# Two-layer hybrid encoder step: most gate products of the merge taken in pairs by seven half products instead of eight

## The chip, the cores and the metric

The kernel runs on one core of one Trainium2 chip. The metric is the device time of one execution in microseconds (us), the median of several runs.

## The reference

One step of a streaming encoder with two layers, on 640 tokens (512 of a prompt, 8 samples of 16) of width 1024, everything in fp32. Cut to what matters here:

```
z = x @ w_in            # 54 blocks of 128 columns are used feature-major below
oa = gelu(u) * (mix_w @ v + b) * silu(a_g)      # chunked spatial gating
ob = rglru(conv4(b_x)) * silu(b_g)              # gated linear recurrence
oc = latent_attention(...) * silu(c_g)
om = memory_attention(m_q, mem_k, mem_v)
g = sigmoid(gate_logits)                        # 4 x 1024 columns of z
merged = g0 * (oa @ w_a) + g1 * (ob @ w_b) + g2 * (oc @ w_c) + g3 * (om @ w_m)
x = layer_norm(ALPHA * x + merged @ w_out)
```

The sigmoid is computed as 0.5 * (1 + tanh(0.5 * logit)). The gate logits are 32 of the 54 column blocks of a layer, each a product of 1024 by 128 weights with 1024 by 640 activations.

## The kernel before

**Arithmetic.** Every large operand is split into two reduced-precision parts, h and lo: ACT casts it (line 145), DVE subtracts the cast from the original (line 146). Each product then takes three matmuls per 128 rows of the contraction: h with h, h with lo, lo with h. `fm_product` (line 116) issues them, each for the two halves of the 640 tokens (TH = 320 columns). A gate chunk thus has 8 x 3 x 2 = 48 matmuls of 128 x 320, all issued at line 120.

**Weights.** `wload` (line 108) sends a DMA from SP's queue into a tile `raw` (three slots of 1024 columns), and ACT and DVE split it into `wh` and `wl` (two slots for each size).

**Order of work in a layer.** Projections `c` and `v`, keys and values of the memory (`mem_kv`, line 210), q, k and v of the attention, attention with the mixing of the gating branch placed among its matmuls (line 623), memory attention, the recurrence (lines 734 to 799: convolution, gates, scan), then the merge, then the output projection (line 953) and the layer norm. A scheduler fills each engine's queue at build time from the order of the code and of the tile slots; an engine runs its queue strictly in order. Waits arise from tiles: a write waits for the readers of the slot or tile, and a tile counts as one, also where two operations touch different halves of it.

**The merge** (`merge`, line 853) runs over the branches oa, oc, ob and om, and in each over 8 output blocks f. For each f: `fm_chunk` (48 matmuls), tanh on ACT (line 865), the branch's own product `y` (24 matmuls of 320 columns, 12 for om), then on DVE the product of gate and branch (lines 877 and 881). For the second to fourth branch it is added to the sum `macc` (line 884), by POOL for oc and ob and by DVE for om. The first four chunks of oa are interleaved with the recurrence. The lines that set the merge's order:

```
for f in range(8):
    o = fm_chunk(22 + br * 8 + f)
    g = ftmp([128, T], "g")
    ACT.activation(out=halves(g), in_=o, func=AF.Tanh, scale=0.5)
    wh, wl = wload(ins["w_brm"][l, f] if br == 3 else ins["w_br"][l, br, f], nk * 128)
```

Of the kernel before, what the change touches and what calls it, by code (L numbers as in the profile page):

```python
# [16 lines left out]
D = 1024  # L17
# [23 lines left out]
def encoder_step(  # L41
# [19 lines left out]
    def xtile(name):  # L61
        return xp_.tile([128, 4, T], F32R, tag="x", name=name)
# [40 lines left out]
    def wraw(src, n=1024):  # L103
        raw = wp.tile([128, n], F32, tag="raw", name="raw", bufs=3)
        nc.sync.dma_start(out=raw, in_=src)
        return raw

    def wload(src, n=1024):
        raw = wraw(src, n)
        sz = "" if n > 512 else "2"  # L110
        h = wp.tile([128, n], F32R, tag="wh" + sz, name="wh")
        lo = wp.tile([128, n], F32R, tag="wl" + sz, name="wl")
        split(h, lo, raw)
        return h, lo

# [12 lines left out]
    def tm_products(outs_, lhs_h, lhs_l, nc_, nk_per, width, load):  # L128
        for ci in range(nc_):
            wh, wl = load(ci)  # L130
            steps = [(j, a, wh) for j in range(nk_per) for a in (lhs_h, lhs_l)]
            steps += [(j, lhs_h, wl) for j in range(nk_per)]
            for n, (j, a, w) in enumerate(steps):
                for t, o in enumerate(outs_):
                    PE.matmul(  # L135
                        out=o[:, 0:width],
                        lhsT=a(ci * nk_per + j)[:, t * 128:(t + 1) * 128],
                        rhs=w[:, j * width:(j + 1) * width],
                        start=(ci == 0 and n == 0),
                        stop=(ci == nc_ - 1 and n == len(steps) - 1),  # L140
                    )
# [33 lines left out]
    xscr = dr.tile([T, D], F32, name="xscr")  # L175

    for l in range(L):
# [12 lines left out]
        mh = kvtile([128, KD, 256], F32R, "mem_h")  # L190
        ml = kvtile([128, KD, 256], F32R, "mem_l")
        def mem_in(k):
            mt = wraw(ins["memT"][:, k:k + 4, :].rearrange("p a b -> p (a b)"))
            for m in range(2):
                split(
                    mh[:, k + 2 * m:k + 2 * m + 2, :], ml[:, k + 2 * m:k + 2 * m + 2, :],
                    mt[:, m * 512:(m + 1) * 512].rearrange("p (a b) -> p a b", a=2),
                )

        def w_mem(c):  # L200
            r = wload(ins["w_mem"][l, c])
# [42 lines left out]
        def w_c(c):  # L244
            if l > 0:
                return wload(ins["w_c"][l, c], 832)
            if c > 0:
                r = wload(ins["w_c"][l, c], 832)
                x_in(2 * c, 2)
                return r  # L250
            raw = wp.tile([128, 832], F32, tag="raw", name="raw", bufs=3)
            h = wp.tile([128, 832], F32R, tag="wh", name="wh")
            lo = wp.tile([128, 832], F32R, tag="wl", name="wl")
            for j in range(2):
                js = slice(416 * j, 416 * j + 416)
                nc.sync.dma_start(out=raw[:, js], in_=ins["w_c"][l, c][:, js])
                x_in(j, 1)
                split(h[:, js], lo[:, js], raw[:, js])
            return h, lo
# [7 lines left out]
        def fm_chunk(c, l=l):  # L267
            h, lo = wload(ins["w_fm"][l, c])
            o = acc("fm")
            fm_product(  # L270
                o,
                lambda k: h[:, k * 128:(k + 1) * 128],
                lambda k: lo[:, k * 128:(k + 1) * 128],
                xhk, xlk, KD,
            )
            return o[:, :, 0:TH]

# [29 lines left out]
        def w_v(c):  # L307
            r = wload(ins["w_v"][l, c])
# [46 lines left out]
        sc = stile([128, 5120], F32, "sc")  # L355
        ckvT_s = sc[:, 0:1152].rearrange("p (b k) -> p b k", b=NB)
        krT_s = sc[:, 1152:2304].rearrange("p (b k) -> p b k", b=NB)
        past = sc[:, 2304:3328].rearrange("p (b k) -> p b k", b=NB)
        qa = sc[:, 3328:4352].rearrange("p (b k) -> p b k", b=NB)
        qrs = sc[:, 4352:4864].rearrange("p (b k) -> p b k", b=NB)  # L360
# [3 lines left out]
        nc.sync.dma_start(out=past, in_=ins["past_ckv"][l].rearrange("b k c -> k b c"))  # L364

# [59 lines left out]
        def q_product(o, wh, wl, m):  # L425
            fm_product(
                o,
                lambda k: wh[:, (2 * m + k) * 128:(2 * m + k + 1) * 128],
                lambda k: wl[:, (2 * m + k) * 128:(2 * m + k + 1) * 128],
# [3 lines left out]
        wh, wl = wload(ins["w_uqr"][l], 512)  # L433
# [17 lines left out]
        wh, wl = wload(ins["w_uqn"][l])  # L451
# [18 lines left out]
        wh, wl = wload(ins["w_ukv"][l])  # L470
        for hp in range(4):
            o = bank_s("k_ps")
            ms = slice(hp * 128, (hp + 1) * 128)
            for n, (a, b) in enumerate(((wh, ckh), (wl, ckh), (wh, ckl))):
                PE.matmul(out=o, lhsT=a[:, ms], rhs=b, start=(n == 0), stop=(n == 2))
# [3 lines left out]
        for t in range(4):  # L479
            o = bank_s("v_ps")  # L480
            ts_ = slice(t * 128, (t + 1) * 128)
            for n, (a, b) in enumerate(((ckh, wh), (ckh, wl), (ckl, wh))):
                PE.matmul(out=o, lhsT=a[:, ts_], rhs=b[:, 512:1024], start=(n == 0), stop=(n == 2))
            (DVE.tensor_copy if t % 2 else ACT.copy)(out=vc[:, t, :], in_=o)

# [72 lines left out]
        for i in range(4):  # L558
# [42 lines left out]
            )  # L601

# [1 line left out]
        for c in range(4):  # L604
# [4 lines left out]
        wmx = stile([128, 1536], F32, "wmx")  # L609
        ws_p = wmx[:, 0:512].rearrange("p (g q) -> p g q", g=4)  # L610
        ws_s = wmx[:, 512:1024].rearrange("p (g q) -> p g q", g=4)
        bs = wmx[:, 1024:1536].rearrange("p (g q) -> p g q", g=4)
        nc.sync.dma_start(out=wmx[:, 0:1024], in_=ins["w_mix"][l])
        nc.sync.dma_start(out=wmx[:, 1024:1536], in_=ins["rows"][l:l + 1, 1024:1536].partition_broadcast(128))
        wm = wmx[:, 0:1024].rearrange("p (g q) -> p g q", g=8)
        POOL.affine_select(
            out=wm, in_=wm, pattern=[[0, 8], [1, 128]],
            compare_op=ALU.is_ge, fill=0.0, base=0, channel_multiplier=-1,
        )
        for c in range(4):  # L620
            o = acc("mix").rearrange("p a b -> p (a b)")
            for t in range(NT):
                PE.matmul(  # L623
                    out=o[:, t * 128:(t + 1) * 128], lhsT=v[:, t, c * 128:(c + 1) * 128],
                    rhs=(ws_p if t < 4 else ws_s)[:, c, :], start=True, stop=True,
                )
            th = ftmp([128, T], "mixb")
            DVE.tensor_tensor(
                out=th[:, 0:NP_].rearrange("p (a b) -> p a b", a=4),
                in0=o[:, 0:NP_].rearrange("p (a b) -> p a b", a=4),  # L630
                in1=bs[:, c:c + 1, :].to_broadcast([128, 4, 128]), op=ALU.add,
            )
            DVE.tensor_tensor(
                out=th[:, NP_:T].rearrange("p (a b) -> p a b", a=NB),
                in0=o[:, NP_:T].rearrange("p (a b) -> p a b", a=NB),
                in1=bs[:, c:c + 1, 0:TS].to_broadcast([128, NB, TS]), op=ALU.add,
            )
            DVE.tensor_tensor(out=oa[:, c, :], in0=oa[:, c, :], in1=th, op=ALU.mult)
# [142 lines left out]
        def lru_rest(c):  # L781
# [17 lines left out]
            DVE.tensor_tensor(out=obs, in0=obs, in1=samp(lb[c % 2][:, 1, :])[:, :, 0:TS], op=ALU.mult)  # L799

# [49 lines left out]
        macc = atile([128, 8, T], F32, "macc")  # L850
        mgh, mgl = [], []

        def merge(bi):
            src, nk, scale = ((oa, 4, 0.5), (oc, 4, 0.5), (ob, 4, 0.5), (om, 2, 1.0))[bi]
            br = (0, 2, 1, 3)[bi]
            bhl = stile([128, 2, nk, T], F32R, "bhl")
            for k in range(nk):
                split(bhl[:, 0, k, :], bhl[:, 1, k, :], src[:, k, :], scale)
            if bi == 3:
                mgh.extend(otile([128, 4, T], F32R, f"mgh{i}") for i in range(2))  # L860
                mgl.extend(otile([128, 4, T], F32R, f"mgl{i}") for i in range(2))
            for f in range(8):
                o = fm_chunk(22 + br * 8 + f)
                g = ftmp([128, T], "g")
                ACT.activation(out=halves(g), in_=o, func=AF.Tanh, scale=0.5)  # L865
                wh, wl = wload(ins["w_brm"][l, f] if br == 3 else ins["w_br"][l, br, f], nk * 128)
                y = acc("y")
                fm_product(
                    y,
                    lambda k: wh[:, k * 128:(k + 1) * 128],  # L870
                    lambda k: wl[:, k * 128:(k + 1) * 128],
                    lambda k: bhl[:, 0, k, :], lambda k: bhl[:, 1, k, :], nk,
                )
                y = y[:, :, 0:TH]
# [233 lines left out]
```

## Time and profile before

| | |
|---|---|
| device time, median of 3 runs (lowest, highest) | 1449.41 us (1448.57, 1450.07) |
| span of the profiled execution, first to last instruction | 1446.2 us |
| median over that span | 3.2 us |
| granted TensorE clock over the span | 0.998 of full |
| busy share PE, PE weight loads, DVE, ACT, POOL | 99%, 91%, 49%, 37%, 10% |
| share of PE in the chain that ended last | 93% |
| DMA, mean | 93 GB/s |

PE is the matmul engine TensorE, DVE is VectorE, ACT ScalarE, POOL GpSimd, SP SyncE, whose queue issues most DMAs. A busy PE says only that matmuls were in flight: they are pipelined, so what one costs is the distance between two starts, not its own duration. The chain that ended last is followed back from the last instruction to what released each step.

### The profile page before, as it was taken

Reading aid. Unit: us, or ns where it says so; the run is one execution under the profiler, and the core shown is the slowest. Engines: PE = TensorE matmul, PEld = TensorE weight load, DVE = VectorE, ACT = ScalarE, POOL = GpSimd, SP = SyncE. Lnnn points to the kernel's source line nnn. Section 1 sums busy time; section 2 is a strip of 40 time slices with the busy share of each in tenths; the row PEclk is TensorE's granted clock in tenths of the full one; section 3 lists DMA queues with packets and bytes.
Section 4 is the critical chain, followed back from the end, with each engine's and each line's share of the span. In section 5 each row is a group of like instructions: output and inputs, shape, how many; then the busy total and the mean of one; then the engine's idle time right before and its main releaser. Section 6 shows DMA issues by size and latency. Waiting matters only on the chain.

```text
span 1446.2 us, 22712 instructions
## 1 busy us (share of the span) xinstructions
PE 1426.0 (99%) x9376; PEld 1322.8 (91%) x9376; DVE 709.0 (49%) x1264; ACT 530.9 (37%) x931; POOL 138.7 (10%) x200
## 2 busy tenths in 40 slices
PE   8999999999999999999999999999999999999997
PEld 8899888989999999998898998788899999999986
DVE  5643577386542232444834535763954322323546
ACT  5533443265532232333234434432664222222320
POOL 2020000010101112100111100000111011211000
PEclk9999999999999999999999999999999999999999
DMA  8342113213222222134372222032132222222323
GB/s 288 115 142 74 52 36 111 78 59 111 74 80 73 81 73 77 61 101 156 115 229 92 85 73 66 30 117 81 48 121 69 73 81 73 81 64 73 114 73 110
DMA packets 51065, 134.16 MB, mean 93 GB/s; under 512 B 5777, under 2 KB 14897, under 8 KB 49937
## 3 DMA queue, kind: packets, MB, share of 16 engines
q1 hardware_dynamic: 49328, 127.54, 27.7%
q0 software_dynamic: 1632, 5.16, 1.0%
q8 instruction: 74, 1.21, 0.4%
q14 instruction: 31, 0.25, 0.1%
HBM read 123.59 MB, written 7.78 MB: 91 GB/s over the span
## 4 chain that ended last, share of the span: by engine, by line
PE 93%; DVE 4%; ACT 1%; DMA 1%; issue 1%; DVEq 0%; POOL 0%; SPq 0%; ACTq 0%
PE fm L120 52%; PE y L120 14%; PE y_ps L953 6%; PE v L135 4%; PE c L135 3%; PE sc_ps L568 3%; PE pv_ps L592 2%; PE mem L135 2%; PE q_ps L120 1%; PE pt_ps L585 1%; PE gate L773 1%; PE mix L623 1%; PE ss_ps L513 1%; DVE wl L146 1%; PE ptm_ps L831 1%
## 5 line engine op out<-in xcount | busy, mean ns | idle before, releaser
L146 DVE TENSOR_TENSOR wl<-raw,wh 128x1024 fp32r<-128x1024 f32 (+4 forms) x203 | 206.0, 1016 | 419.4 <-issue 288.8
L120 PE MATMUL fm<-xh,wh 128*128 128x320 f32 x1728 | 406.9, 313 | 0.0
L120 PE MATMUL fm<-xl,wh 128*128 128x320 f32 x1728 | 404.1, 312 | 0.0
L145 ACT CAST wh<-raw 128x1024 fp32r<-128x1024 f32 (+4 forms) x203 | 179.2, 883 | 477.6 <-PE fm L120 326.8
L120 PEld LDWEIGHTS fm<-xh,wh 128*128 128x128 f32 x1728 | 289.3, 188 | 8.3 <-issue 5.0
L120 PEld LDWEIGHTS fm<-xl,wh 128*128 128x128 f32 x1728 | 289.6, 188 | 5.6 <-issue 4.9
L120 PE MATMUL fm<-xh,wl 128*128 128x320 f32 x1728 | 281.0, 311 | 0.0
L120 PEld LDWEIGHTS fm<-xh,wl 128*128 128x128 f32 x1728 | 258.7, 188 | 3.4 <-issue 2.6
L120 PE MATMUL y<-bhl,wh 128*128 128x320 f32 x896 | 141.6, 309 | 0.0
L120 PEld LDWEIGHTS y<-bhl,wh 128*128 128x128 f32 x896 | 133.6, 188 | 0.0
L884 POOL TENSOR_TENSOR macc<-macc,g 128x640 f32<-128x640 f32 x32 | 62.1, 1941 | 340.5 <-DVE g L881 340.5
L881 DVE SCALAR_TENSOR_TENSOR g<-g,y 128x640 f32<-128x640 f32 x48 | 39.4, 821 | 95.8 <-PE y L120 95.8
L120 PE MATMUL y<-bhl,wl 128*128 128x320 f32 x448 | 76.6, 309 | 0.0
L865 ACT ACTIVATE g<-fm 128x640 f32<-128x640 f32 x64 | 45.2, 706 | 81.4 <-PE fm L120 81.3
L120 PEld LDWEIGHTS y<-bhl,wl 128*128 128x128 f32 x448 | 68.3, 188 | 0.0
L568 PE MATMUL sc_ps<-kT,qT 128*128 128x128 f32 (+7 forms) x128 | 45.6, 450 | 0.0
L577 ACT ACTIVATE p_c<-sc_ps,mx 128x128 f32<-128x128 f32 (+3 forms) x64 | 33.6, 532 | 4.5 <-DVE mx L574 4.5
L953 PE MATMUL y_ps<-wo,mgh 128*128 128x512 f32 x120 | 35.1, 396 | 0.0
L587 ACT COPY pt_c<-pt_ps 128x128 f32<-128x128 f32 (+3 forms) x32 | 13.6, 425 | 52.8 <-PE pt_ps L585 52.8
L574 DVE TENSOR_REDUCE mx<-sc_ps 128x1 f32<-128x128 f32 (+3 forms) x64 | 30.3, 477 | 0.5
L585 PE MATMUL pt_ps<-ident,p_c 128*128 128x128 f32 x160 | 28.4, 275 | 1.7 <-DVE pt_c L587 1.7
L585 PEld LDWEIGHTS pt_ps<-ident,p_c 128*128 128x128 f32 x160 | 19.9, 140 | 10.8 <-issue 4.3
(295 smaller groups left out, 1675.2 us busy)
## 6 DMA issues: line engine op xcount, KB each, us to landing
raw<-in_w_fm SPq DMA_DIRECT2D x108, 512.0 KB, 3.5
raw<-in_w_br SPq DMA_DIRECT2D x48, 256.0 KB, 2.6
mcache<-in_mem_kv SPq DMA_DIRECT2D x8, 1024.0 KB, 4.8
raw<-in_w_out SPq DMA_DIRECT2D x16, 512.0 KB, 4.3
raw<-in_w_v SPq DMA_DIRECT2D x8, 512.0 KB, 4.0
raw<-in_w_mem SPq DMA_DIRECT2D x8, 512.0 KB, 3.5
raw<-in_w_c SPq DMA_DIRECT2D x7, 416.0 KB, 5.1
xr<-in_x SPq DMA_DIRECT2D x10, 256.0 KB, 3.0
```

The source lines that it names most:

```text
L120: PE.matmul(out=out[:, j, 0:TH], lhsT=a(k), rhs=b(k)[:, j * TH:(j + 1) * TH], start=(n == 0), stop=(n == len(steps) - 1),)
L135: PE.matmul(out=o[:, 0:width], lhsT=a(ci * nk_per + j)[:, t * 128:(t + 1) * 128], rhs=w[:, j * width:(j + 1) * width], start=(ci == 0 and ...
L145: ACT.copy(out=dst_h, in_=src)
L146: DVE.tensor_tensor(out=dst_l, in0=src, in1=dst_h.bitcast(F32), op=ALU.subtract)
L568: PE.matmul(out=s[:, 0:nk], lhsT=qT[0:kr_, h, ts_], rhs=kT[h // 4][0:kr_, h % 4, 0:nk], start=True, stop=True,)
L574: DVE.tensor_reduce(out=mx, in_=s[:, 0:nk], axis=AX.X, op=ALU.max, negate=True)
L577: ACT.activation(out=p[:, 0:nk], in_=s[:, 0:nk], func=AF.Exp, bias=mx, accum_out=sm)
L585: PE.transpose(tps[:, k * 128:(k + 1) * 128], p[:, k * 128:(k + 1) * 128], ident)
L865: ACT.activation(out=halves(g), in_=o, func=AF.Tanh, scale=0.5)
L881: DVE.scalar_tensor_tensor(out=halves(g), in0=halves(g), scalar=1.0, in1=y, op0=ALU.add, op1=ALU.mult)
L884: (POOL if bi < 3 else DVE).tensor_tensor(out=m, in0=m, in1=g, op=ALU.add)
L953: PE.matmul(out=o[j], lhsT=a[k // 4][:, k % 4, t * 128:(t + 1) * 128], rhs=w[:, j * 512:(j + 1) * 512], start=(k == 0 and p == 0), stop=(k ...
```

## The change

The gate chunks 4 to 7 of oa and all of oc, ob and om (28 of 32 in a layer) are computed two at a time by `fm_pair` (line 309 of the changed kernel). Two chunks form a 2 x 2 block matrix: the rows are the two chunks, the columns the two halves of the contraction (4 x 128 each). The activations form another: halves of the contraction by halves of the tokens. Instead of eight half products (each 12 matmuls of 320 columns) it makes seven, from sums of weight blocks (`wsum`, 4 DVE additions of 512 columns for a pair) and of activation blocks (`x_sums` and `x_sum_in_place`, DVE, once a layer, in the recurrence's stage), and five DVE operations of 320 columns on the results in PSUM (lines 356, 358, 362, 364 and 367).

```
         def fm_pair(c, take):
             a11, a12, a21, a22 = (
                 wraw(ins["w_fm"][l, c + e][:, i * 512:(i + 1) * 512]) for e in range(2) for i in range(2)
             )
...
+            product(ba, a11, 11, True, False)
+            ACT.copy(out=p1, in_=ba)
+            s1 = wsum(a21, a22, "ws1")
+            s2 = wsum(a11, s1, "ws2")
+            product(bb, s2, 2, True, True)
+            DVE.tensor_tensor(out=u, in0=p1, in1=bb, op=ALU.subtract)
+            product(bc, wsum(a11, a21, "ws3"), 3, True, False)
+            DVE.tensor_tensor(out=z1[:, hi_], in0=bc, in1=u, op=ALU.subtract)
+            product(ba, a12, 21, False, True)
+            take(0, lo_, ba)
+            product(bd, s1, 1, True, False)
+            DVE.tensor_tensor(out=z1[:, hi_], in0=z1[:, hi_], in1=bd, op=ALU.subtract)
+            product(bc, a22, 4, False, True)
+            DVE.tensor_tensor(out=z1[:, lo_], in0=bc, in1=u, op=ALU.subtract)
+            take(1, slice(0, T), z1)
+            product(bd, wsum(a12, s2, "ws4"), 22, False, True)
+            DVE.tensor_tensor(out=z0[:, hi_], in0=bd, in1=u, op=ALU.add)
+            take(0, hi_, z0[:, hi_])
```

`product` splits its weight block (ACT cast, DVE subtraction, 512 columns) and issues 12 matmuls. `ba` and `bb` lie in one PSUM tile, `bc` and `bd` in another.

The other edits: the weights come in pieces of 512 columns and 256 KB (`raw` six slots, `wh` and `wl` four each, sums `ws` four); the addition to `macc` is on DVE for all branches; oc, ob and om are written to DRAM by DMAs from SP's queue (`spill`) and read back for their branch's first pair (`back`, tile `osrc`); activations, branch results and others share one pool of ten slots; the output projection's weights are loaded in halves; and the mixing moves from the attention to the stage ahead of the q products.

```
+    def spill(bi, k, src):
+        nc.sync.dma_start(out=oscr[bi][k], in_=src)
...
+        def x_sums():
...
+            for k in range(4):
...
+                x_sum1(k, t1, t2)
+                DVE.tensor_tensor(out=t2, in0=t1, in1=b22[0], op=ALU.add)
+                DVE.tensor_tensor(out=t2, in0=t2, in1=b22[1], op=ALU.add)
+                split(xt[2][0][:, k, :], xt[2][1][:, k, :], t2)
+                DVE.tensor_tensor(out=t4, in0=b21[0], in1=t2, op=ALU.subtract)
+                DVE.tensor_tensor(out=t4, in0=t4, in1=b21[1], op=ALU.add)
+                split(xt[4][0][:, k, :], xt[4][1][:, k, :], t4)
+                DVE.tensor_tensor(out=t3, in0=b12[0], in1=b22[0], op=ALU.subtract)
+                DVE.tensor_tensor(out=t1, in0=b12[1], in1=b22[1], op=ALU.subtract)
+                DVE.tensor_tensor(out=t3, in0=t3, in1=t1, op=ALU.add)
+                split(xt[3][0][:, k, :], xt[3][1][:, k, :], t3)
+                yield
...
+        ma = merge_whole()
+        bhl = next(ma)
         lru_gates(1)
         lru_rest(1)
+        xs_ = x_sums()
+        next(xs_)
...
+        x_sum_in_place()
+        merge_pairs(0, (4, 6), bhl)
         for bi in (1, 2, 3):
-            run_some(merge(bi), 9)
+            merge_pairs(bi, (0, 2, 4, 6))
```

**The queues in a pair.** On PE, in the merge before, 48 matmuls of a gate chunk (`fm`) and 24 of a branch product (`y`) alternate. These are the last rows of one chunk and the branch product behind it:

```order
L120 MATMUL fm<-xh_0_98,wl 128x320 x8
L120 MATMUL fm<-xh_1_99,wl 128x320 x8
L120 MATMUL y<-bhl,wh 128x320 x16
L120 MATMUL y<-bhl,wl 128x320 x8
```

On PE now, in a pair of the branch oa, from the end of the product of s2 with its activation sum (xt_3650) to the product of a22 (xt_3652); the rows left out are the eight `wh` matmuls of the products of a12 (xh_1) and of s1 (xh_0):

```order
L344 MATMUL fp<-xt_3650,wl 128x320 x4
L344 MATMUL fp<-xt_3651,wh 128x320 x4
L344 MATMUL fp<-xt_3651,wl 128x320 x4
...
L344 MATMUL fp<-xh_1_100,wl 128x320 x4
...
L344 MATMUL fp<-xh_0_99,wl 128x320 x4
L123 MATMUL y<-bhl_3513,wh 128x320 x2
L123 MATMUL y<-bhl_3514,wh 128x320 x2
L123 MATMUL y<-bhl_3513,wh 128x320 x2
L123 MATMUL y<-bhl_3514,wh 128x320
L344 MATMUL fp<-xt_3652,wh 128x320 x8
L344 MATMUL fp<-xt_3652,wl 128x320 x4
```

Between the end of s2's product and the first matmul of a22's stand 8 + 12 + 12 + 7 = 39 matmuls. In the pairs of om there are 35, since s3's product is divided 6 and 6 there, and the branch product 5. The product of a22 writes the tile of `bc` and `bd`, so it waits for the DVE operation of line 362, which reads `bd`.

On DVE now, in a pair of oc, from the operation `u` (line 356, behind s2's product) to line 362; names as in `fm_pair`, where the two `ws` rows are ws1 and ws2 of the pair that follows:

```order
L356 TENSOR_TENSOR tu<-tu,fp 128x320
L149 TENSOR_TENSOR wl<-raw,wh 128x512
L358 TENSOR_TENSOR z_5044<-fp,tu 128x320
L149 TENSOR_TENSOR wl<-ws_5153,wh 128x512
L149 TENSOR_TENSOR wl<-raw,wh 128x512
L333 TENSOR_TENSOR ws_5271<-raw 128x512
L333 TENSOR_TENSOR ws_5273<-raw,ws_5271 128x512
L362 TENSOR_TENSOR z_5044<-z_5044,fp 128x320
```

In that place stood, for each chunk before, two splits and one product of gate and branch. Now the `wl` behind `u` is the last reader of the raw tile of this pair's a22, and the sums of the next pair's weights, which need its a21 and a22, stand ahead of line 362.

On SP stand, for each pair, four DMAs of gate pieces and two of branch pieces, for six `raw` slots; so the DMA of a pair's a22 waits for the slot of the a22 before it. In the first pair of oc, ob and om, the reads of the branch result stand on SP between the third and the fourth gate piece, and on DVE three of its four splits (line 152) stand where ws1 and ws2 stand above; the two of om (line 149) stand ahead of ws1.

On ACT in layer 0, the copies of `mem_kv` out of PSUM, with the semaphores they wait for, first as they stood before and then as they stand now. DVE and the other engines' names are their instruction counters, DMASW is a DMA of POOL's queue, DMAHW one of SP's:

```order
L220 COPY mkv_618<-mem 128x512 [waits DMASW0_49]
L220 COPY mkv_619<-mem 128x512 [waits DVE_49]
```

```order
L224 COPY mkv_691<-mem 128x512 [waits DMASW0_49]
L148 CAST wh<-raw 128x512 [waits DMAHW7_49,PE_49,Activation_49]
L224 COPY mkv_692<-mem 128x512 [waits DMASW2_49,Activation_49,Pool_49]
L148 CAST wh<-raw 128x512 [waits DMAHW0_49,DVE_49,PE_49]
L232 COPY mem<-mkT_ps 128x512 [waits PE_49]
```

The second copy now takes the slot of the first, and waits for the DMA that writes the first copy out.

## Rows read from the trace of the kernel before

**Rows 1.** The page's head: span, then busy time, share and instructions of each engine

```profile
span 1446.2 us, 22712 instructions
PE 1426.0 (99%) x9376; PEld 1322.8 (91%) x9376; DVE 709.0 (49%) x1264; ACT 530.9 (37%) x931; POOL 138.7 (10%) x200
```

**Rows 2.** The page's chain that ended last: share by engine, by line

```profile
PE 93%; DVE 4%; ACT 1%; DMA 1%; issue 1%; DVEq 0%; POOL 0%; SPq 0%; ACTq 0%
PE fm L120 52%; PE y L120 14%; PE y_ps L953 6%; PE v L135 4%; PE c L135 3%; PE sc_ps L568 3%; PE pv_ps L592 2%; PE mem L135 2%; PE q_ps L120 1%; PE pt_ps L585 1%; PE gate L773 1%; PE mix L623 1%; PE ss_ps L513 1%; DVE wl L146 1%; PE ptm_ps L831 1%
```

**Rows 3.** Chain, merges and output projection: start us, us, what, matmuls

```profile
394.00 7.04 PE fm L120 x48
401.04 3.51 PE y L120 x24
...
612.10 7.04 PE fm L120 x48
619.14 1.75 PE y L120 x12
...
1383.44 55.00 PE y_ps L953 x240
```

**Rows 4.** Work by stretch: us, busy time (instructions) of each engine, clock, DMA share, GB/s

```profile
333.00:394.00 61.00, 60.84 (x420) 59.63 (x419) 33.06 (x41) 36.20 (x49) 7.50 (x17) 1.00 0.33 102
394.00:665.00 271.00, 271.00 (x1850) 270.96 (x1850) 96.30 (x136) 74.00 (x98) 32.55 (x19) 1.00 0.26 81
```

**Rows 5.** Instruction groups of DVE by shape: busy us, mean ns of one, idle before

```profile
L146 DVE TENSOR_TENSOR wl<-raw,wh 128x1024 fp32r<-128x1024 f32 x128 | 156.8, 1226 | 398.4 <-issue 288.8 <-PE fm L120 70.6 <-PE v L135 22.4
L146 DVE TENSOR_TENSOR wl<-raw,wh 128x512 fp32r<-128x512 f32 x50 | 34.4, 688 | 3.3 <-ACT wh L145 3.3
L146 DVE TENSOR_TENSOR wl<-raw,wh 128x256 fp32r<-128x256 f32 x16 | 6.7, 417 | 0.0
L884 DVE TENSOR_TENSOR macc<-macc,g 128x640 f32<-128x640 f32 x16 | 13.1, 820 | 0.1
L599 DVE TENSOR_TENSOR oc<-pv_ps,oc 128x512 f32<-128x512 f32 x8 | 5.5, 692 | 2.6 <-PE pv_ps L592 2.4
```

**Rows 6.** Timeline of DVE, SP and PE at two chunks: start us, us, what

```profile
404.66 0.82 DVE L877 SCALAR_TENSOR_TENSOR macc<-g,y 128x640 f32<-128x640 f32 x1 [1.87 <-PE y L120]
404.83 0.31 PE L120 MATMUL fm<-xl,wh 128*128 128x320 f32 x1
...
405.40 0.68 DVE L146 TENSOR_TENSOR wl<-raw,wh 128x512 fp32r<-128x512 f32 x1
...
411.69 1.22 DVE L146 TENSOR_TENSOR wl<-raw,wh 128x1024 fp32r<-128x1024 f32 x1 [5.60 <-issue]
...
412.94 0.33 SPq L105 DMA_DIRECT2D raw<-in_w_br  x1
```

**Rows 7.** Chain where PE waited for DVE in the recurrence: start us, us, what

```profile
377.77 3.53 PE y L120 x24
381.30 0.03 issue
381.33 0.02 DVEq L877
381.35 0.04 issue
381.39 0.83 DVE macc L877
382.23 0.04 issue
382.27 1.18 PE gate L773 x6
```

**Rows 8.** DMA issues: queue, count, KB each, median us to landing

```profile
raw<-in_w_fm SPq DMA_DIRECT2D x108, 512.0 KB, 3.5
raw<-in_w_br SPq DMA_DIRECT2D x48, 256.0 KB, 2.6
xr<-in_x SPq DMA_DIRECT2D x10, 256.0 KB, 3.0
xr<-xscr SPq DMA_DIRECT2D x10, 256.0 KB, 3.5
```

**Rows 9.** The mixing's matmuls in layer 0's chain: start us, us, what, matmuls

```profile
213.97 0.89 PE mix L623 x8
...
230.29 0.67 PE mix L623 x6
```

**Rows 10.** Operations on mkv, layer 0: times ns, starts us; us to landing

```profile
L223 PE MATMUL mkT_ps<-ident,mkv x4: 272/273/327, 73.3 to 75.6; 128*128 128x128 f32 x4
L220 ACT COPY mkv<-mem x2: 588/589/590, 72.6 to 74.6; 128x512 f32<-128x512 f32 x2
L221 POOL DMA_DIRECT2D out_mkv<-mkv x2: 540/556/572, 73.5 to 75.5; - x2
DMA to landing us min/median/max: 2.3/3.8/5.2
```

More of the change, by code (lines that the diff above doesn't have):

```diff
@@ L175, in encoder_step @@
     xscr = dr.tile([T, D], F32, name="xscr")
+    oscr = [dr.tile([4, 128, T], F32, name=f"oscr{i}") for i in range(4)]
+    def spill(bi, k, src):
+        nc.sync.dma_start(out=oscr[bi][k], in_=src)
     for l in range(L):
@@ new lines, in x_sum_in_place, with fm_pair, wsum, product @@
+        def x_sum_in_place():
+            xt[1] = xh[0][:, :, hi_], xl[0][:, :, hi_]
+            for k in range(4):
+                t_ = tmp([128, T], "t1")
+                x_sum1(k, t_[:, lo_], t_[:, hi_])
+                split(xt[1][0][:, k, :], xt[1][1][:, k, :], t_[:, lo_])
+        def fm_pair(c, take):
+            a11, a12, a21, a22 = (
+                wraw(ins["w_fm"][l, c + e][:, i * 512:(i + 1) * 512]) for e in range(2) for i in range(2)
+            )
+            def wsum(a, b, name):
+                o = wtile("ws", 512, name, 4)
+                DVE.tensor_tensor(out=o, in0=a, in1=b, op=ALU.add)
+                return o
+            ab, cd = acc("fp"), acc("fp")
+            ba, bb, bc, bd = (o[:, j, 0:TH] for o in (ab, cd) for j in range(2))
+            def product(o, w, x, first, last):
+                h, lo = whl(w)
+                bh, bl = xt[x]
+                steps = [(k, h, b) for k in range(4) for b in (bh, bl)] + [(k, lo, bh) for k in range(4)]
+                for n, (k, a, b) in enumerate(steps):
+                    PE.matmul(
+                        out=o, lhsT=a[:, k * 128:(k + 1) * 128], rhs=b[:, k, :],
+                        start=(first and n == 0), stop=(n == len(steps) - 1), skip_group_check=True,
+                    )
+            z0, z1, t_ = ftmp([128, T], "z0"), ftmp([128, T], "z1"), tmp([128, T], "tu")
+            p1, u = t_[:, lo_], t_[:, hi_]
+            product(ba, a11, 11, True, False)
[16 more added lines that the diff above has]
+            take(0, hi_, z0[:, hi_])
+            return z0, z1
@@ L604, in encoder_step @@
         for c in range(4):
+            spill(2, c, oc[:, c, :])
+        for c in range(4):
             th = ftmp([128, T], "sga")
             silu_into(th, FM_AG + c)
-            DVE.tensor_tensor(out=oa[:, c, :], in0=oa[:, c, :], in1=th, op=ALU.mult)
[L609 to L637, printed above, removed]
             DVE.tensor_tensor(out=oa[:, c, :], in0=oa[:, c, :], in1=th, op=ALU.mult)
@@ L850, in encoder_step @@
         macc = atile([128, 8, T], F32, "macc")
[L851 to L856, printed above, removed]
-            for k in range(nk):
-                split(bhl[:, 0, k, :], bhl[:, 1, k, :], src[:, k, :], scale)
-            if bi == 3:
[L860 to L863, printed above, removed]
+        mg = []
@@ L885, in merge, with merge_pairs, back @@
-                if bi == 3:
-                    split(mgh[f // 4][:, f % 4, :], mgl[f // 4][:, f % 4, :], m, 0.5)
-                yield
-        def run_some(gen, n):
-            for _ in range(n):
-                next(gen, None)
+                merge_y(0, f, g, bhl)
+                yield bhl
+        def merge_pairs(bi, fs, bhl=None):
+            br = (0, 2, 1, 3)[bi]
+            def back(k):
+                src = tmp([128, T], "osrc")
+                nc.sync.dma_start(out=src, in_=oscr[br][k])
+                return src
+            for f in fs:
+                gs = []
+                z = fm_pair(22 + br * 8 + f, lambda e, cols, v_: gs.append((e, cols, v_)))
+                for e, cols, v_ in gs:
+                    ACT.activation(out=z[e][:, cols], in_=v_, func=AF.Tanh, scale=0.5)
+                if bhl is None:
+                    bhl = bsplit(bi, back)
+                if bi == 3:
+                    mg.append(otile([128, 2, 2, T], F32R, f"mg{f}"))
+                for e in range(2):
+                    merge_y(bi, f + e, z[e], bhl)
```

224 lines of the change are left out of this document (141 added, 83 removed).

## The prediction

> **What bounds the kernel now.** I read the page's head first, then the chain, then the stretches. PE is busy 99% of the span, at a granted clock that is full [rows 1, 4], and PE work makes 93% of the chain; of it the gate and projection matmuls (fm) make 52% and the branch products (y) 14% [rows 2]. In the merge the chain is nothing but the two alternating on PE: 7.04 us for 48 matmuls, 3.51 for 24, 1.75 for 12 [rows 3]. So matmuls of 320 columns start 7.04 / 48 = 0.1467 us apart, and PE has no gap there: 271.00 us busy in 271.00, while DVE works 96.3 and ACT 74.0 [rows 4]. A removed matmul returns its 0.1467 us only as long as DVE, ACT and the DMAs deliver in time. The sum is made against the profiled execution, a span of 1446.2 us; the median of the runs is 3.2 us longer, and I let these 3.2 us stand. About 0.2% (2.9 us) is what a measurement can tell from no change.
>
> **What it removes.** 14 pairs in each of two layers, with 84 matmuls in place of 96: 28 x 12 x 0.1467 = **49.3 us** of PE work. The products now write one bank 12 times in a row; the output projection does so with 512 columns at 55.00 / 240 = 0.229 us each, no more per column, so I keep 0.1467 [rows 3].
>
> **What it adds in a pair.** From its splits, DVE's two-operand operation costs 417, 688 and 1226 ns at 256, 512 and 1024 columns, so 0.15 us and 1.05 ns a column, and 0.485 us at 320; the next may start 0.08 us before its end (404.66 + 0.82 against 405.40) [rows 5, 6]. Reading PSUM adds nothing: 692 against 688 ns [rows 5]. A pair of oa, oc or ob holds DVE for 13 operations of 512 (four sums, seven gate and two branch splits) at 0.61, five of 320 at 0.41 and four of 640 at 0.74: 12.9 us beside 108 + 24 = 132 matmuls or 19.4 us of PE. With om it is about 13.8 beside 108 x 0.1467 = 15.8. This lies beside PE, and so do ACT's nine casts. What doesn't is one ring through four queues. The last gate piece, a22, of the next pair can be loaded only when this pair's a22 is split; that split stands behind `u`, which waits for the product of s2; and the sums ws1 and ws2, which wait for that load, stand ahead of line 362, on which this pair's a22 product waits. From the end of s2's product:
>
> - the last matmul's result, 0.31 - 0.15 = 0.16 [rows 6], and PE to DVE, 0.09 (381.30 to 381.39) [rows 7]
> - `u`, 0.41, and the split, 0.69 [rows 5]
> - DVE to SP, 0.03 (411.69 + 1.22 to 412.94) [rows 6]
> - the load of 256 KB: 2.6, 3.0 and 3.5 in three rows [rows 8]; I take 2.8, between the branch weights, which come from the same queue into the same kind of slot but one at a time, and the rows of x
> - its link to DVE, 0.04, as DVE to PE [rows 7]; ws1 0.69, ws2 0.61, line 362 0.49, the link to PE 0.04
>
> That is 6.05 us. PE meanwhile has 39 matmuls, 5.72 us, in 20 of the pairs and 35, 5.13 us, in the 8 of om. So it stops for 0.33 and 0.92: 20 x 0.33 + 8 x 0.92 = **+14.0**. With 2.6 it would be 8.4, with 3.5 it would be 33.6. The six pairs that read a branch back have splits of 640 in that place (three, 2.2 us, for ws1 and ws2's 1.3, or two ahead of ws1 in om); I leave them in the count. The granted clock stays full at such stops: beside 1 us waits in the recurrence it reads 1.00 [rows 4, 7].
>
> One rule of the skill speaks against this part. The rows show that at 512 columns DVE takes 692 ns from PSUM and 688 from SBUF [rows 5]. The Trainium skill, VectorE: DVE Perf Modes, section The TRN2 errata, says that each operation pays a fixed latency, so that tiles should hold 512 elements or more, and its table gives a source in PSUM 62 cycles at 0.96 GHz more than one in SBUF. By that, an estimate from the page, `u` and line 362 would each be 0.065 us longer and the ring 28 x 0.13 = 3.6 us dearer, 1436.7 in place of 1433.1; these rows do not bear the surcharge out, while the fixed part they show is 0.15 us.
>
> **The recurrence's stage.** Here DVE gains 52 operations of 320 (`x_sums`) and 16 (`x_sum_in_place`) a layer, 68 x 0.41 = 27.6 us, in a stretch of 61 us in which it already works 33.1 [rows 4]: 60.7 of 61. PE there already waits for DVE ahead of its gate matmuls (381.30 to 382.27) [rows 7]. Nothing is left over to make up a late gate. Bounds: 0, if the sums fall exactly into the gaps; 27.6 / 2 = 13.8 a layer, if only half does. I take 5, since the in-place sums (6.5) come last and the first pairs need them: **+10**.
>
> **The mixing.** Its matmuls fill PE while the softmax runs: six pieces in the chain of layer 0, 4.5 us [rows 9]. Ahead of the q products they cost PE the same 4.5, and one wait for DVE as in the recurrence, 0.97 [rows 7]. In the attention between 0 and 4.5 come back, as the softmax then has less to hide behind; I take 2.2. 2 x (4.5 + 1.0 - 2.2) = **+6.6** (2 to 11).
>
> **The slot of mkv.** In layer 0 the second copy waits for the write of the first, issued at 73.5 and landed 2.3 to 5.2 us later, 3.8 in the middle. Then comes a copy of 0.59 and a link, and PE's transposes, which stood at 75.6 [rows 10], start at 78.0: **+2.4** (0.9 to 3.8).
>
> **At nothing**: the spills and reads (20 of 320 KB a layer, beside 81 GB/s [rows 4]; without that cover 0.33 us of SP's queue each, 13 us in all), loads in halves (the same bytes; one more issue of 0.33 us [rows 6] for a chunk of 7.04 us of PE), the output projection's loads (under the last pairs), POOL's additions now on DVE (in the 12.9).
>
> **The sum**: -49.3 + 14.0 + 10 + 6.6 + 2.4 = -16.3, a span of 1429.9, and 1433.1 us with the 3.2: I say **1433**.
>
> **The rivals.**
> 1. *The loads come later* (slower). Four pieces and two branch pieces now share the queue; rows of 256 KB land in 3.5 [rows 8]. Against it: DMA carries 81 GB/s there, with 0.26 of its engines' time [rows 4]. At 3.5 the ring costs 33.6 and the time is 1453; from there 0.1 us costs 2.8, so 3.8 gives 1461. The gain is gone from 2.8 + 16.3 / 28 = 3.4 us on. Chance 0.13.
> 2. *DVE is the bound.* If an operation of 320 columns takes as long as one of 512, `u` and line 362 lengthen the ring by 0.4, 28 x 0.4 = 11: 1444; with om's 13.8 of 15.8 us no slack is left either. Against it, the three sizes lie on one line [rows 5]. Chance 0.11.
> 3. *The waits are hidden.* If the ring takes 5.5 us, the pairs of oa, oc and ob lose nothing and om 8 x 0.37 = 3.0; with the sums in the gaps, 1449.4 - 49.3 + 3.0 + 6.6 + 2.4 = 1412. For it: the best such load lands in 2.6. Chance 0.13.
> 4. *The matmuls do not get fewer in time*: a product whose 12 matmuls go to one bank runs slower than 0.1467. At 0.16, 28 x 84 x 0.013 = 31 us return, 1464. The output projection speaks against it [rows 3]. Chance 0.03.
>
> **How the numbers follow.** The forecast, with its own range of 1424 to 1442 from the bounds of the load and the smaller terms, has 0.60. The range of 1416 to 1450 takes in rival 2 and the upper part of rival 3, and leaves out most of rivals 1 and 4 and the rest of 3, about 0.2. Faster by over 0.2%: 0.60, rival 3's 0.13, nearly all of rival 2, together 0.82; within it 0.05, the near side of rival 1 and the far side of 2; slower 0.13, the rest of rival 1 and rival 4.
>
> **What would show it.** In the profile after: 2352 matmuls of `fp` at 0.147 apart; in each pair one stop of PE ahead of the a22 product, released by DVE line 362, 0.3 us long and 0.9 in om; ws1 released by the DMA of a raw tile; DVE near full in the recurrence, with PE waiting there; PE waiting for mkv near 76 us. I am wrong if PE has no stop there (rival 3), if stops are over 1 us (rival 1), or if `fp` starts lie further apart (rival 4).

## The result, and the profile after

The changed kernel takes 1434.31 us (median of 4 runs, 1432.02 to 1434.48) against 1449.31 us of the kernel before on the same chip: a ratio of 0.9896, with a 95% interval of 0.9882 to 0.9910, or 15.0 us less. The forecast was 1433, in a range of 1416 to 1450. The sum came out; three of its terms did not, and their errors cancelled.

The page's head and its chain, by engine and by line, after:

```profile
span 1432.4 us, 23820 instructions
PE 1396.3 (97%) x9040; PEld 1276.1 (89%) x9040; DVE 989.5 (69%) x1919; ACT 628.2 (44%) x1254; POOL 74.4 (5%) x168
PE 85%; DVE 8%; DMA 2%; ACT 2%; issue 2%; POOL 0%; DVEq 0%; SPq 0%; ACTq 0%
PE fm L123 24%; PE fp L344 21%; PE y L123 12%; PE y_ps L1084 7%; PE v L138 4%; PE c L138 3%; PE sc_ps L693 3%; PE pv_ps L717 2%; PE mem L138 2%; PE pt_ps L710 1%; DVE wl L149 1%; DMA raw<-in_w_fm 1%; PE q_ps L123 1%; ACT wh L148 1%; PE gate L870 1%
```

PE has 336 matmuls fewer than before (9040 against 9376) [rows 1], as counted: 28 x 12. Its share of the chain falls from 93 to 85% [rows 2] and DVE's rises from 4 to 8: the bound is still PE, but no longer PE alone.

Work by stretch after: first the recurrence's stage of layer 0, from its first gate matmul to the first pair, then the pairs; and the same two in layer 1 (columns as in rows 4):

```profile
307.70:388.35 80.65, 75.45 (x522) 71.60 (x521) 75.99 (x142) 51.04 (x98) 9.27 (x23) 0.98 0.21 69
388.40:662.00 273.60, 268.08 (x1766) 259.16 (x1765) 205.17 (x357) 120.66 (x211) 2.90 (x6) 1.00 0.33 104
1019.70:1100.25 80.55, 75.38 (x522) 71.53 (x521) 75.88 (x142) 51.05 (x98) 9.22 (x23) 0.98 0.22 69
1100.30:1371.30 271.00, 266.38 (x1762) 258.18 (x1761) 200.22 (x328) 119.82 (x209) 2.91 (x6) 1.00 0.34 105
```

DVE is busy 76.0 of 80.65 us in the recurrence's stage and 205 of 273.6 in the pairs, where it had 96 of 271 [rows 4]. The granted clock reads 0.98 in the recurrence, where it was 1.00.

The same stage before, with the same 522 matmuls, from the first gate matmul to the first one behind the last:

```profile
308.05:383.28 75.23, 74.22 (x522) 70.01 (x521) 49.22 (x70) 45.53 (x80) 9.36 (x23) 1.00 0.29 89
```

It has grown by 5.4 us a layer. The chain in two pairs of oc (start us, us, what; compare rows 3):

```profile
481.70 1.99 PE fp L344 x12
483.69 0.73 PE y L123 x5
484.42 1.88 PE fp L344 x12
486.30 5.28 PE y L123 x36
491.58 8.99 PE fp L344 x60
500.57 1.03 PE y L123 x7
501.59 0.02 issue
501.62 2.02 PE fp L344 x12
```

A pair takes 501.62 - 481.70 = 19.92 us, where its 132 matmuls need 19.36. Twelve matmuls need 1.76: the product of a22 (1.99, 2.02) and that of ws4 (1.88) take longer, and the five products that stand in a row 8.99 for 8.80. Those are the stops.

What PE waited for, over the whole span (us in total, times, longest; the lines of the gates and the pairs):

```profile
PE gate L870 <- DVE macc L970: 6.5, 4, 2.2
PE y L123 <- DVE z L367: 3.2, 6, 0.5
PE fp L344 <- DVE tu L356: 2.8, 2, 1.4
PE fp L344 <- DVE z L362: 2.3, 7, 0.6
```

In the pairs of om the chain shows another place:

```profile
604.00 1.77 PE fp L344 x12
605.80 0.50 DVE z L367
606.44 2.00 PE y L123 x12
```

The second branch product waits for line 367, the last reader of the PSUM tile whose slot it takes. From the distances of all matmul starts in the pairs of both layers, what lies above 0.1467 us adds up to 25.8 us: 7.5 at a22's product in the pairs of oa, oc and ob (line 362), 5.1 at s2's product in all pairs, 2.3 at ws4's in the pairs of oa, oc and ob, 6.6 at other places in om's pairs and at their end (4.6 of it at the second branch product), 4.1 at other places in the two first pairs, and 0.3 ahead of branch products.

### The profile page after: what moved, and what is told of

It reads as the page before. It is cut to its first block, busy times and chain, and to the rows that moved or that the text cites. A ratio compares the mean times of both kernels' runs of the same rounds, so it can differ in the third digit from the quotient of the medians.

```text
span 1432.4 us, 23820 instructions
## 1 busy us (share of the span) xinstructions
PE 1396.3 (97%) x9040; PEld 1276.1 (89%) x9040; DVE 989.5 (69%) x1919; ACT 628.2 (44%) x1254; POOL 74.4 (5%) x168
## 4 chain that ended last, share of the span: by engine, by line
PE 85%; DVE 8%; DMA 2%; ACT 2%; issue 2%; POOL 0%; DVEq 0%; SPq 0%; ACTq 0%
PE fm L123 24%; PE fp L344 21%; PE y L123 12%; PE y_ps L1084 7%; PE v L138 4%; PE c L138 3%; PE sc_ps L693 3%; PE pv_ps L717 2%; PE mem L138 2%; PE pt_ps L710 1%; DVE wl L149 1%; DMA raw<-in_w_fm 1%; PE q_ps L123 1%; ACT wh L148 1%; PE gate L870 1%
## 5 line engine op out<-in xcount | busy, mean ns | idle before, releaser
L148 ACT CAST wh<-raw 128x512 fp32r<-128x512 f32 (+1 forms) x310 | 187.1, 605 | 375.4 <-PE fp L344 125.2
L149 DVE TENSOR_TENSOR wl<-raw,wh 128x512 fp32r<-128x512 f32 (+1 forms) x310 | 209.0, 677 | 186.2 <-PE fm L123 83.2
L123 PE MATMUL fm<-xh,wh 128*128 128x320 f32 x832 | 209.6, 324 | 0.4 <-DVE oc L528 0.2
L123 PE MATMUL fm<-xl,wh 128*128 128x320 f32 x832 | 199.6, 316 | 0.0
L123 PEld LDWEIGHTS fm<-xh,wh 128*128 128x128 f32 x832 | 141.9, 190 | 9.0 <-issue 5.1
L123 PEld LDWEIGHTS fm<-xl,wh 128*128 128x128 f32 x832 | 140.9, 190 | 5.7 <-issue 4.5
L123 PE MATMUL fm<-xh,wl 128*128 128x320 f32 x832 | 141.4, 315 | 0.0
L344 PE MATMUL fp<-xh,wh 128*128 128x320 f32 x448 | 135.7, 315 | 3.6 <-DVE tu L356 2.8
L344 PE MATMUL fp<-xl,wh 128*128 128x320 f32 x448 | 133.0, 309 | 0.0
L123 PEld LDWEIGHTS fm<-xh,wl 128*128 128x128 f32 x832 | 125.2, 188 | 4.0 <-issue 3.9
```

Source lines behind the costliest of these rows:

```text
L123: PE.matmul(out=out[:, j, 0:TH], lhsT=a(k), rhs=b(k)[:, j * TH:(j + 1) * TH], start=(n == 0), stop=(n == len(steps) - 1),)
L148: ACT.copy(out=dst_h, in_=src)
L149: DVE.tensor_tensor(out=dst_l, in0=src, in1=dst_h.bitcast(F32), op=ALU.subtract)
L344: PE.matmul(out=o, lhsT=a[:, k * 128:(k + 1) * 128], rhs=b[:, k, :], start=(first and n == 0), stop=(n == len(steps) - 1), skip_group_chec ...
```

## The experiments

**Four banks for the four accumulators.** `ba` and `bb` share a PSUM tile of two banks, and so do `bc` and `bd`; these tiles come from the same two slots as the branch product's. Four other banks are idle in the pairs.

```
-            ab, cd = acc("fp"), acc("fp")
-            ba, bb, bc, bd = (o[:, j, 0:TH] for o in (ab, cd) for j in range(2))
+            ba, bb, bc, bd = (
+                o[:, 0:TH] for o in (bank_s("fp"), bank_t("fp"), bank_s("fp"), bank_o("fp"))
+            )
```

> The four accumulators of a pair (ba, bb, bc, bd) each get a PSUM tile of one bank, from the banks that are idle in the pair stage, so that the two double tiles serve the branch products alone. Theory (PE stops because two accumulators share a tile, so that a product waits for a reader of its neighbour, and because a branch product waits for that tile): the stops at s2's product (5.0 us in both layers), at a22's (7.4), at the ws4 product (2.4) and at om's second branch product (5.7) go, 20.5 us in all, about 1414 us; only the first pair of a layer still stops. Rival (DVE, ACT and the loads set the pace in a pair, and the stop only moves to another product): at most 5 us less, 1429 or more.

1410.63 us (1410.42 to 1411.42), a ratio of 0.9734 (0.9719 to 0.9748) to the kernel before: 23.7 us less than the changed kernel, and the fastest of the runs that leave nothing out. Its chain in a pair of oc:

```profile
447.64 12.32 PE fp L345 x84
459.96 7.04 PE y L123 x48
```

84 matmuls in 12.32 us are 0.1467 each, without a stop, and this in one bank twelve times in a row. So 0.1467 was the right price for a product, and the stops belonged to the shared tiles. DVE, ACT and the loads keep up with PE at full speed there. Counted as above, 9.4 us are left in the pairs of both layers, 16.5 less, and 3.7 a layer of them lie in the first pair. The theory had 20.5, so part of the 23.7 has another source, which was not expected: the last six gate matmuls of a layer, and PE's wait ahead of them, now stand behind the first two matmuls of the first pair, and the stage up to that pair takes 76.9 us in each layer in place of 80.7. Some 0.9 us of that is work that only moved.

**Two banks for one side at a time.** `ba` and `bb` alone:

```
-            ab, cd = acc("fp"), acc("fp")
-            ba, bb, bc, bd = (o[:, j, 0:TH] for o in (ab, cd) for j in range(2))
+            cd = acc("fp")
+            ba, bb, bc, bd = bank_s("fp")[:, 0:TH], bank_t("fp")[:, 0:TH], cd[:, 0, 0:TH], cd[:, 1, 0:TH]
```

> Only ba and bb get a bank of their own. Theory: the stop of s2's product behind ACT's copy of ba goes (5.0 us); s2's product also moves 4 matmuls ahead and PE has 42 matmuls (6.16 us) up to a22's product for the ring of 6.05, so the stops there shrink from 0.3 to about 0.1 (4 to 6 us less); om's stops stay. About 1424 us. Rival (the 0.1 us behind each stop belongs to the first matmuls on a new bank, not to a wait): no stop of 0.1 goes, 1432 or more.

1422.02 us (1420.16 to 1423.26): 12.3 less. Five products in a row now take their 8.80 us:

```profile
488.58 8.80 PE fp L344 x60
497.38 0.88 PE y L123 x6
498.26 1.97 PE fp L344 x12
```

The stop of s2's product is gone, so it was ACT's copy of `ba`, a read of the neighbour in the tile. The stop ahead of a22's product (1.97 for 1.76) did not shrink as expected, although PE has three matmuls more up to it. The trace says why. In the changed kernel the load is what ws1 waits for: in the ordinary pairs ws1 starts 0.09 us behind the load's landing (479.71 and 479.80 in the pair above). In this run the load lands at 495.97, and ws1 stands on DVE behind a split that waits for ACT's cast:

```profile
495.72 0.69 DVE L149 TENSOR_TENSOR wl<-raw,wh 128x512 fp32r<-128x512 f32 x1 [0.74 <-ACT wh L148]
496.33 0.68 DVE L333 TENSOR_TENSOR ws<-raw 128x512 f32<-128x512 f32 x1
```

So a22's product now waits for DVE's queue order and no longer for the load. The rest of the gain lies in the recurrence and the first pairs (80.7 to 78.4 us from the gates to the first pair in layer 0, 80.6 to 76.9 in layer 1), and that part I had not expected. Here too the last six gate matmuls stand behind the first two of the pairs, so 0.9 us a layer of it only moved; and in the first pair a12's product no longer waits for line 356, which reads `bb`, its neighbour in the tile (1.4 us in each layer in the list of waits above).

`bc` and `bd` alone, with the same edit on the other side:

```
+            ab = acc("fp")
+            ba, bb, bc, bd = ab[:, 0, 0:TH], ab[:, 1, 0:TH], bank_s("fp")[:, 0:TH], bank_o("fp")[:, 0:TH]
```

> Only bc and bd get a bank of their own. Theory: a22's product needs no line 362 any more, which has 12 matmuls and more until the ws4 product; the stops at a22 (7.4), ws4 (2.4) and om's branch product (5.7) go, s2's stays: about 1419 us. Rival (the ring of load, split and sums is the pace of the pair by itself, whatever PE may do meanwhile): the stop moves to the ws4 product, 1431 or more.

1417.21 us (1415.95 to 1417.57): 17.1 less, 15.5 expected. In the ordinary pairs only s2's stop is left, 12.52 for 12.32:

```profile
448.27 12.52 PE fp L344 x84
```

Line 362 stands in the same place on DVE as before, behind ws1 and ws2 of the next pair. It now has until the ws4 product, and that is enough. The ring is no pace by itself: it cost only because a22's product waited for a reader of `bd`, which it does not touch.

**The ring cut in another way.** The products of a22 and s1 change places, within the shared tiles:

```
+            product(bc, a22, 4, False, True)
+            DVE.tensor_tensor(out=z1[:, lo_], in0=bc, in1=u, op=ALU.subtract)
             product(bd, s1, 1, True, False)
             DVE.tensor_tensor(out=z1[:, hi_], in0=z1[:, hi_], in1=bd, op=ALU.subtract)
-            product(bc, a22, 4, False, True)
-            DVE.tensor_tensor(out=z1[:, lo_], in0=bc, in1=u, op=ALU.subtract)
```

> Within a pair the products of a22 and of s1 change places, so that a22 is split ahead of u and its load for the next pair no longer waits for s2's product. Theory (the ring of split, load and sums makes the stop ahead of a22's product in the pairs of oa, oc and ob): the ring is cut, the stops there go, 7 us less with those of s2's product and of om left: 1427. Rival (those stops are DVE's backlog alone, whatever the load): the stop moves to s1's product and the time stays at 1433 or more.

1430.78 us (1429.34 to 1430.98): 3.5 less, between the two expectations. In the ordinary pairs the a22 stop is gone; at s1's product 0.1 us is left of 0.2 to 0.4, and pairs that read a branch back keep 0.3. The ring of the prediction is real, but half of what was counted at it is the shared tile.

**The mixing where it was.** The mixing's matmuls and sums are placed behind the attention again:

> The mixing's matmuls and sums stand behind the attention's again (its loads stay ahead). The prediction's price (moving them cost 3.3 us a layer): 6.6 us less, 1427.7. Theory from the two traces (what the q stage lost, the attention gave back): no change, within 1.5 us of the changed kernel's 1434.3.

1470.71 us (1468.14 to 1473.24): 36.4 more, which neither theory had. The queue order explains it only in part: in layer 0 the mixing stands at 181.9 to 194.1 us, ahead of the attention of the eight samples, which starts at 195.9 in place of 152.8, and the load of that attention's scratch tile waits for it:

```profile
SPq L554 <- PE mix L719: 22.6, 2, 13.3
```

That tile comes from the shared pool and could get its slot only when the mixing's weights gave theirs up; this reading is from the trace and was not tried apart. PE is busy 45.6 of the 58 us from 142 to 200 there, at a granted clock of 0.85, where the changed kernel has 57.9 at 1.00. As a test of the price the run says nothing, so the next two measure it by leaving the mixing out.

**Without the mixing**, in the changed kernel and in the kernel before; both drop the block of `acc("mix")`, its matmuls, sums and the product with oa:

> Leaves out the mixing of the gating branch (20 matmuls, their sums and the product with oa in each layer) from the changed kernel; its loads stay. Both: PE loses 4.5 us a layer and one wait of about 1 ahead of the q products, and nothing hides them there: 9 to 11 us less, 1423 to 1425.

> Leaves out the same from the kernel before, where it stood among the attention's matmuls. The prediction's price (half of it filled waits of the softmax and comes back as waits): 4.4 us less, 1445. Theory from the traces (the attention gave back all that the q stage lost): as much as in the changed kernel, 9 us or more, 1440 or less.

1423.24 us (1421.68 to 1426.88) and 1437.61 us (1437.55 to 1438.46): 11.1 less than the changed kernel and 11.6 less than the kernel before. It costs the same in both places, within the spread of the runs; up to the start of the memory attention, the traces of both layers together have 11.0 us less without it in the kernel before and 12.5 in the changed one. The attention of the kernel before had no wait for it to fill; in that stage without the mixing (148 to 281 us):

```profile
148.00:281.00 133.00, 133.00 (x951) 111.34 (x950) 79.35 (x223) 53.04 (x137) 2.92 (x8) 1.00 0.22 72
```

PE is busy 133.00 of 133.00: other chunks move up and stand between the softmax's steps. So they do in the changed kernel's attention:

```profile
207.04 1.03 PE fm L123 x7
208.07 0.33 PE pt_ps L710 x3
```

**Lighter activation sums.** The low parts are left out of them (32 of 68 operations of 320 columns a layer), so that the gates are products of less exact activations:

> Leaves the low parts of the activations out of the activation sums: 32 of 68 DVE operations of 320 columns a layer, 13 us of DVE in the recurrence's stage. Theory (a full DVE makes PE's gate matmuls and first pair late, some 5 us a layer): 8 to 10 us less, 1424 to 1426. Rival (those waits come from the recurrence's own chain of DVE, ACT and POOL, and the sums lie in its gaps): less than 2 us, 1432 or more.

1429.81 us (1424.81 to 1432.24): 4.5 less, between the two, and with a wide spread. The gate stops in the recurrence stay (PE waits 2.4 us for line 964 there, 3.3 in the changed kernel).

**Banks for the gates too.** A gate product takes one of the two double tiles, whose reader in the branch product's place (line 970) stands on DVE behind the recurrence and the sums. In this run the gate products of the last three of a layer's four blocks get single banks, and their tanh two halves; the pairs have the four banks as above:

```
-                o = acc("gate")
...
+                    og = [t_[:, 0:half] for t_ in (
+                        (bank_s("gate"), bank_s("gate")) if m == 0 else (bank_t("gate"), bank_o("gate"))
+                    )]
```

> The four single banks for the pairs as before, and for the gates of the recurrence's last three blocks too, each tanh on ACT in two halves. Theory (in the recurrence PE stops 2 to 3 us at a time because a gate product takes the tile of a branch product, whose reader stands behind the activation sums on DVE; behind the longest of these stops the granted clock is low for 3.4 us in each layer): the gate stops of 3.3 us a layer go, the clock stays at its upper level, 1.7 us a layer; 1400 to 1404 us. Rival (the gates are late by the recurrence's own chain on a full DVE, and PE only waits elsewhere): no less than 1408.

1412.19 us (1411.18 to 1413.12), no better than the banks for the pairs alone: the rival. The waits for line 970 are gone and the clock reads 1.00 in that stage, yet the stage and the pairs together are hardly shorter than with the pairs' banks alone (339.0 and 338.8 us in the two layers, against 340.1 and 338.9); PE stops elsewhere:

```profile
PE fm L123 <- ACT g L992: 1.9, 1, 1.9
PE fp L345 <- ACT lb L882: 1.8, 1, 1.8
```

The second of these waits for the recurrence's own tanh and exponential, which come late. With the lighter sums on top:

> The same, and it leaves the low parts of the activations out of the activation sums (13 us of DVE a layer). Theory: with the gate stops gone, what the sums cost is the first pair's wait and little else, 2 to 5 us less than the run with the banks alone. Rival (DVE is the bound of the recurrence's stage): 8 us less or more.

1400.54 us (1400.31 to 1401.69): 11.7 less, the rival again. 13 us less DVE a layer give 5.8 back. Once PE's tiles are out of the way, DVE bounds the recurrence's stage, at 74.8 of 80.3 us.

**Part of the sums on POOL.** 24 of the 68 operations a layer go to POOL, which is idle there (9 of 80 us busy):

```
-                x_sum1(k, t1, t2)
+                x_sum1(k, t1, t2, POOL)
...
-                DVE.tensor_tensor(out=t3, in0=b12[0], in1=b22[0], op=ALU.subtract)
+                POOL.tensor_tensor(out=t3, in0=b12[0], in1=b22[0], op=ALU.subtract)
```

> The single banks, and 24 of the activation sums' 68 operations a layer on POOL in place of DVE. Theory (the recurrence's stage is bound by DVE, where 13 us less a layer gave 5.8): 24 x 0.41 = 9.8 us less DVE a layer give 3 to 4.5, so 1402 to 1405 us. Rival (POOL's operations, about 1 us each, come late or hold DVE up where they run beside it): 1410 or more.

> The same with the single banks for the gates. Theory: the gates' banks pay only once DVE has room; 1400 to 1403 us. Rival as in the run with the banks alone: 1410 or more.

1433.23 us (1432.10 to 1433.35) and 1429.81 us (1429.36 to 1431.67): 22.6 and 17.6 more than the same without it. Groups of POOL and of DVE in the run with the pairs' banks, DVE's in the recurrence's stage (308 to 400 us), and, last, the same DVE group without POOL:

```profile
L313 POOL TENSOR_TENSOR t<-xl,xl 128x320 f32<-128x320 f32 x8 | 9.9, 1236 | 16.2 <-DVE t L306 16.2
L291 POOL TENSOR_TENSOR t<-xh 128x320 f32<-128x320 f32 x8 | 8.5, 1060 | 7.5 <-PE mo_ps L939 7.5
L149 DVE TENSOR_TENSOR xt<-t,xt 128x320 fp32r<-128x320 f32 x12 | 9.6, 819 | 0.0
```

```profile
L149 DVE TENSOR_TENSOR xt<-t,xt 128x320 fp32r<-128x320 f32 x12 | 6.7, 573 | 0.0
```

POOL needs 1.0 to 1.24 us where DVE needs 0.48, and DVE's own operations grow beside it, 573 to 819 ns. PE's longest waits in the recurrence's stage are now these, one of each in a layer (over the span, in the first of the two runs; without POOL the longest there was 2.2):

```profile
PE gate L871 <- DVE macc L971: 11.3, 2, 5.6
PE y L123 <- ACT lb L841: 10.3, 2, 5.4
```

The granted clock is 0.989 over the span, where it was 0.996 without POOL. The Trainium skill, SBUF — State Buffer, section Who interferes with whom, states that a DVE instruction with two inputs in SBUF contends with a GpSimd instruction that reads SBUF, and that the port pair the two share is an exclusive lock. The longer means of DVE beside POOL agree; no run here shows which of the two waited.

## Why the prediction was right, point by point

**The PE work** (-49.3 us) held exactly: 336 matmuls fewer, and 0.1467 us for each `fp` matmul where nothing stops it. That rules out the fourth rival.

**The ring** was priced at 14.0 us, the stops of the pairs measured 25.8. In the pairs of oa, oc and ob the step held: ws1 was released by the load, as foretold, and 0.33 a stop was forecast, 6.6 in all, and 7.5 measured. That they lie so close is in part luck: 2.0 of the 7.5 are the 0.10 us behind each stop that the last section tells of, which the sum did not have. The load took 2.7 us in the median (2.8 was taken) and the two PSUM operations of 320 columns 487 and 480 ns (485):

```profile
L356 DVE TENSOR_TENSOR tu<-tu,fp 128x320 f32<-128x320 f32 x28 | 13.6, 487 | 33.9 <-ACT wh L148 31.4 <-PE fp L344 2.2
L291 DVE TENSOR_TENSOR t<-xh 128x320 f32<-128x320 f32 x16 | 7.7, 481 | 0.0
raw<-in_w_fm SPq DMA_DIRECT2D x216, 256.0 KB, 2.7
```

With the load at 2.7 the first rival is out, the second with the 0.48. The surcharge of 0.065 us for a source in PSUM, which the prediction had worked out from the table of the Trainium skill (VectorE: DVE Perf Modes, The TRN2 errata), does not show here: 487 ns from PSUM stand against 481 from SBUF. In om the step failed: not one long stop stands ahead of a22's product. There line 362 stands ahead of ws1 on DVE, where the prediction had kept oc's order, so there is no ring through the load:

```profile
617.31 0.49 DVE L362 TENSOR_TENSOR z<-z,fp 128x320 f32<-128x320 f32 x1 [1.21 <-PE fp L344]
...
618.04 0.69 DVE L333 TENSOR_TENSOR ws<-raw 128x512 f32<-128x512 f32 x1
```

In place of the 7.4 us put there om's pairs lose 6.6 at other places, 4.6 of them where the second branch product waits for its PSUM slot. What the sum lacked altogether are waits on PSUM tiles, which "This lies beside PE" passed over: s2's product behind ACT's copy (5.1), ws4's (2.3), and a12's behind line 356 in the first pairs. I had read the false wait at a22 from the tile rule, and did not apply the same rule to the other six products. The runs with separate banks show all of these.

**The recurrence's stage** was put at 10 us. The stage itself grew by 5.4 us in each layer and the first pairs stop 4.1 more, 15 in all, where the 10 was meant to be both. The reason, a full DVE, is borne out where PE's tile waits are out of the way (11.7 us for 26 us of DVE); with them in place the lighter sums gave only 4.5.

**The mixing** (+6.6) was wrong. It costs 11 us before and after, so the move costs next to nothing: the memory attention starts at 280.1 us in layer 0, where it started at 280.4. The step that failed is "the softmax then has less to hide behind": the scheduler put gate and projection chunks there, so the attention gave the whole 4.5 us a layer back.

**The slot of mkv** (+2.4) was wrong too. The wait is there, but the transposes stand later in PE's queue, behind 21 matmuls in place of 13, and start at 75.9 where they started at 75.6 [rows 10]; the q products begin at 85.4 against 85.7.

**Together**: -49.3 + 25.8 + 10.8 + 0 + 0 = -12.7 against a span that is 13.8 shorter; 1.1 stays unexplained, 0.7 of it ahead of the recurrence's stages. The forecast's -16.3 had 12.6 us too little in the pairs and the recurrence and 9 too much in the mixing and mkv. It was right in its range, its sign and its mechanism of the ring, and as near as it was by luck.

## What to carry to other kernels

Two accumulators in one PSUM tile are one thing to the scheduler: count for each product who last read the neighbour, and give accumulators banks of their own when any are idle. Here it was worth 24 us, more than the 15 that the change itself saved. Work that fills waits costs its own time wherever it stands as long as other work can fill the same waits; before pricing a move by the waits it leaves, look for what will move up.

## What the runs showed of the hardware that I had not expected

**A short stop costs 0.10 us more than it lasts.** The product of a22 at 481.7, from the timeline of PE (start us, us, matmuls):

```profile
481.39 0.31 PE L123 MATMUL y<-bhl,wh 128*128 128x320 f32 x1
481.67 0.41 PE L344 MATMUL fp<-xt,wh 128*128 128x320 f32 x1
481.67 0.56 PE L344 MATMUL fp<-xt,wh 128*128 128x320 f32 x2
```

The first matmul behind the wait starts 0.28 us after the last, 0.13 late. It then lasts 0.41 us in place of 0.31, and with the next one 0.56: as that lasts 0.31, it starts 0.25 us after the first, not 0.147. Nearly every stop in the pairs shows it, down to those of 0.09. A likely reason stands in the rows of the weight loads (PEld): a load otherwise starts with the matmul ahead of its own, 0.15 us early, but here none starts with the matmul at 481.39; the load itself waits for line 362 and starts with its own matmul:

```profile
481.10 0.33 PEld L123 LDWEIGHTS y<-bhl,wh 128*128 128x128 f32 x2
481.67 0.19 PEld L344 LDWEIGHTS fp<-xt,wh 128*128 128x128 f32 x1 [0.24 <-DVE z L362]
```

No run tried this apart. Before the change PE had hardly a stop, and no row told of it.

**The clock fell behind a stop.** PE in three stretches of the recurrence's stage, layer 0:

```profile
357.00:360.00 3.00, 2.31 (x16) 2.04 (x14) 3.00 (x6) 0.62 (x1) 0.00 (x0) 1.00 0.33 90
360.00:363.00 3.00, 1.52 (x5) 1.52 (x6) 3.00 (x7) 1.19 (x3) 0.00 (x0) 0.75 0.27 90
363.00:366.00 3.00, 3.00 (x16) 3.00 (x16) 2.27 (x5) 2.69 (x5) 0.00 (x0) 0.68 0.00 0
```

PE stood for 2.2 us behind line 970, and the granted clock went from its upper level, 2.4 GHz, to the lower, 1.2, for part of the two stretches from 360 to 366: (1 - 0.75 + 1 - 0.68) x 3 = 1.7 us of full speed lost, and as much in layer 1. The prediction had said that the clock stays full at such stops, from a wait of 1 us that left it full. It was part of what made the recurrence's stage longer; where the gates had banks of their own, the clock stayed at 1.00. A stop of this length did not always do it. In the run with the pairs' banks PE stood as long at the same place, and the clock stayed at its upper level:

```profile
358.00:361.00 3.00, 0.96 (x7) 0.69 (x5) 3.00 (x7) 0.63 (x2) 0.00 (x0) 1.00 0.56 170
361.00:364.00 3.00, 2.88 (x19) 2.88 (x20) 2.86 (x7) 2.51 (x5) 0.00 (x0) 1.00 0.02 5
```

There it fell behind the next stop, of 1.9 us, at 384.7 to 386.6: from 388 to 391 it reads 0.51. In the run with banks for the gates two stops of 1.9 and 1.8 us left it at 1.00. So these runs show that a stop of about 2 us can cost the clock, and not which one will.
